# An encoder layer on one core: output projection by 1024 columns, with two of eight pairs of k-tiles as seven products of sums

## The chip, the core and the metric

The kernel runs on one core of one Trainium2 chip. The metric is the device time of one execution in microseconds (us), lower is better. Five engines have instruction streams of their own: PE (matrix products), DVE (elementwise, reads PSUM and SBUF), ACT (activations, copies and casts), POOL (elementwise) and SP (it issues the transfers from memory).

## The reference, cut to what matters

One layer of a hybrid encoder on 256 tokens with 2048 features, all float32:

```python
hn = _rmsnorm(h, norm_w[i])
proj = hn @ w_in[i]                      # 2048 x 18432, nine column groups
q, v, f_fwd, f_bwd, z_a, b_gate, c_gate, h_b, z_b = jnp.split(proj, IN_SPLITS, axis=-1)
o_a = _hgrn2_bidirectional(jax.nn.silu(q), v, f_fwd, f_bwd, lb_all[:, i])
o_a = _head_rmsnorm(o_a, hgrn_norm_w[i]) * jax.nn.silu(z_a)
y_b = b_gate * _short_conv(c_gate * h_b, conv_w[i])
o_b = _rmsnorm(y_b, conv_norm_w[i]) * jax.nn.silu(z_b)
h = h + jnp.concatenate([o_a, o_b], axis=-1) @ w_out[i]      # 4096 x 2048, what is changed
gate = jax.nn.sigmoid(h @ w_ple_gate[i])
h = h + (p[i] @ w_ple[i]) * gate
return _rmsnorm(h, final_norm_w)
```

## The kernel before

**Products.** A float32 product is made of three products of `F32R` parts: each operand is split into a high part (a cast) and a low part (the rest), and high x high, high x low and low x high are summed in PSUM. A weight tile of 128 x 1024 numbers (`raw`, from memory) becomes a tile `spl` of both parts: ACT casts it (`split`, L74), DVE subtracts (L75). There are three `raw` buffers and five `spl` buffers. `Stream` holds the list of weight tiles in the order of use; `get(i)` opens and splits tiles up to three ahead of tile i. A transfer into `raw` waits until the splits of the tile that lay there have ended.

**Stages.** Stage A (groups q, v, f, z_a, up to about 500 us): PE runs the input projections; the gated recurrence of two heads at a time (`mix_forgets`, `mix_pair`) goes on beside them on ACT, DVE and POOL, and PE takes in its small products (`scores`, L506 and L550: `scps`, then `cx`). Calls that are due at a later place among PE's products are put off by `at` and made by `tick`. At the start the tokens are loaded a second time, in another layout (`load_tokens`, L261, into the buffer `xf32`); their squares (`x_squares`, L268 on ACT and L269 on DVE) give the norms, which PE spreads over the partitions (`rps`, L284) and DVE copies to `rbc` (L285). All that POOL does for the recurrence begins with a product by `rbc` (`by_norms`, L346).

Stage B (500 to 841 us) is the short convolution: per pair of channel tiles four projections, then POOL multiplies (`cg*hb`, L684) and ACT and DVE split the result into `mixb` (L695, L696). At its end `turn` transposes the last heads into PSUM tiles `ogt` (tags `y` and `x`); ACT and DVE split them into `mixa` (L437, L438).

Output projection: for each j of four groups of 512 columns `gemm_tok` accumulates `pa` (the half from `mixa`, 16 k-tiles, two row blocks of 128 tokens, three products each) and then `pb` (from `mixb`). DVE adds them to `hh`, which starts as the tokens (L758, L762). `h_transposed` brings the new columns into `ht` for the gate. Then, again by 512 columns, `pp` (per-layer embedding) and `pg` (gate), and the last norm.

PSUM has eight banks: four of pool `psg` with the tag `g`, and four of pool `psm` with the tags `x`, `y`, `sc0`, `sc1`. The order of each engine's instructions is set by the framework's list scheduler from the program's order; `high_priority` pulls instructions ahead.

Of the kernel before, what the change touches and what calls it, by code (L numbers as in the profile page):

```python
# [8 lines left out]
F32 = mybir.dt.float32  # L9
# [8 lines left out]
P = 128  # L18
# [9 lines left out]
class Stream:  # L28
# [11 lines left out]
    def add(self, *srcs):  # L40
# [8 lines left out]
        return list(range(first, len(self.where)))  # L49

    def load(self, j, k0=0, k1=None, pool=None):
        srcs, k, n = self.todo[j]
        if j not in self.raws:
            tag = f"raw{j}" if pool else "raw"
            self.raws[j] = (pool or self.rawp).tile([P, 2048], F32, tag=tag, name=f"raw{j}")
        dst = self.raws[j][:, : k * n].rearrange("p (b k n) -> p b k n", b=len(srcs), k=k)
        for b, src in enumerate(srcs):
            self.nc.sync.dma_start(dst[:, b, k0:k1], src[:, k0:k1])

    def open(self, i):  # L60
        j, h = self.where[i]
        srcs, k, n = self.todo[j]
        if j not in self.raws:
            self.load(j)
        part = self.home[i] if i in self.home else self.splp.tile([P, 2048], F32R, tag="spl", name=f"spl{i}")
        self.parts[i] = part.rearrange("p (k s n) -> p k s n", s=2, n=n)
# [22 lines left out]
def tile_hymba_encoder(  # L89
# [20 lines left out]
    splp = ctx.enter_context(tc.tile_pool(name="splp", bufs=5))  # L110
    xsp = ctx.enter_context(tc.tile_pool(name="xsp", bufs=1))
    psg = ctx.enter_context(tc.tile_pool(name="psg", bufs=4, space=PSUM))
# [20 lines left out]
    for i in range(8):  # L133
        for c in (B_CG, B_HB, B_BG, B_ZB):
            blocks[c, i] = sum((ws.add(w_in[c + i, h]) for h in range(2)), [])
    oblocks = [sum((ws.add(w_out[j, h]) for h in range(8)), []) for j in range(4)]
    gblocks, pblocks = [], []
    for j in range(4):
        pblocks.append(ws.add(w_ple[j]))
        if j < 3:  # L140
            gblocks.append(sum((ws.add(w_gate[j, h]) for h in range(4)), []))
        else:
            halves = [[w_gate_end[b, q // 2, :, 4 * (q % 2) : 4 * (q % 2) + 4] for b in range(2)] for q in range(4)]
            gblocks.append(sum((ws.add(*h) for h in halves), []))


# [506 lines left out]
    for i in range(8):  # L653
# [31 lines left out]
        if i == 0:  # L685
# [40 lines left out]

# [12 lines left out]

    def h_transposed(j):  # L740
        for kk in range(2):
            tp = psm.tile([P, 512], F32, tag="xy"[kk], name=f"ht{j}_{kk}")
            kt = 4 * j + 2 * kk
            for k in range(2):
# [4 lines left out]
            tpv = tp.rearrange("p (k t) -> p k t", k=2)  # L749
            act.copy(out=ht[:, kt : kt + 2, 0, :], in_=tpv)  # L750
            dve.tensor_tensor(out=ht[:, kt : kt + 2, 1, :], in0=tpv, in1=ht[:, kt : kt + 2, 0, :], op=ALU.subtract)

    for j in range(4):
        cs = slice(512 * j, 512 * (j + 1))
        pa = [psg.tile([P, 512], F32, tag="g", name=f"pa{j}_{m}") for m in range(2)]
        gemm_tok(pa, oblocks[j][:8], lambda kt, s: mixa[:, kt, s, :])
        for m in range(2):
            dve.tensor_tensor(out=hh[:, m, cs], in0=pa[m], in1=hh[:, m, cs], op=ALU.add)  # L758
        pb = [psg.tile([P, 512], F32, tag="g", name=f"pb{j}_{m}") for m in range(2)]
        gemm_tok(pb, oblocks[j][8:], lambda kt, s: mixb[:, kt, s, :])  # L760
        for m in range(2):
            dve.scalar_tensor_tensor(  # L762
                out=hh[:, m, cs], in0=pb[m], scalar=rb[:, m : m + 1], in1=hh[:, m, cs], op0=ALU.mult, op1=ALU.add
            )
        at(3, lambda j=j: h_transposed(j))


    mctx.close()
    gp = ctx.enter_context(tc.tile_pool(name="gp", bufs=1, side="right", reuse_waits="tile"))
    fw = gp.tile([P, D], F32, name="fw")  # L770
    nc.sync.dma_start(fw, final_norm_w.rearrange("(o d) -> o d", o=1).broadcast_to([P, D]))
# [48 lines left out]
    for j in range(4):  # L820
        cs = slice(512 * j, 512 * (j + 1))
        pp = [psm.tile([P, 512], F32, tag=("sc0", "sc1")[m], name=f"pp{j}_{m}") for m in range(2)]
        gemm_tok(pp, pblocks[j], lambda kt, s: pt[:, kt, s, :])
        pl = []
        for m in range(2):
            t = gp.tile([P, 512], F32, tag="pl", name=f"pl{j}_{m}", bufs=4)
            act.copy(out=t, in_=pp[m])
            pl.append(t)

        def acc(name):  # L830
            return psg.tile([P, 512], F32, tag="g", name=name)

        if j < 3:
# [78 lines left out]
```

## Time and profile before

| | us |
|---|---|
| median of 3 runs (lowest, highest) | 1128.47 (1127.69, 1128.89) |
| the profiled execution's own time | 1127.79 |
| its span, first to last instruction | 1126.1 |
| PE busy in the span | 1116.5 |
| DVE, ACT, POOL busy | 728.5, 629.4, 217.8 |

The profile is of one execution. A busy time is the sum over an engine's instructions; matrix products overlap at their ends, so a product's duration (0.39 us) is longer than its step from start to start. The mean granted TensorE clock was 0.998 of full.

### The profile page before, as it was taken

What the parts mean: (1) busy time and instruction counts of PE and PEld (TensorE: products, weight loads), DVE (VectorE), ACT (ScalarE), POOL (GpSimd) and SP (SyncE); (2) the same over time, 40 slices, a digit from 0 to 9 for tenths busy, and PEclk for the clock granted to TensorE, in tenths of its full rate; (3) what the DMA queues carried; (4) which work ended last, traced back from release to release, by engine and by line L of the source; (5) the groups of instructions that cost most, each with busy time, mean ns of one, the idle gap of its engine ahead of it and who ended that gap; (6) DMA issues with size and microseconds to landing.
All of it is one profiled execution on the core that took longest, in us unless ns stands there. A gap on an engine that the chain in (4) does not pass through costs nothing.

```text
span 1126.1 us, 16341 instructions
## 1 busy us (share of the span) xinstructions
PE 1116.5 (99%) x6530; PEld 959.9 (85%) x6530; DVE 728.5 (65%) x920; ACT 629.4 (56%) x868; POOL 217.8 (19%) x167
## 2 busy tenths in 40 slices
PE   9999999999999999999999999999999999999996
PEld 8888888888888888888888888888888888888886
DVE  7798476956876587766655665565565555545664
ACT  7696577756775586564454454444445434444553
POOL 1144025300622034221121111121220000000112
PEclk9999999999999999999999999999999999999999
DMA  9746445555545455555555565555557555556542
GB/s 352 268 168 209 155 160 188 159 188 181 201 135 209 163 169 169 192 182 187 188 191 187 182 200 196 194 192 192 188 188 270 187 186 187 187 203 212 201 169 75
DMA packets 37371, 214.25 MB, mean 190 GB/s; under 512 B 4144, under 2 KB 4528, under 8 KB 17584
## 3 DMA queue, kind: packets, MB, share of 16 engines
q1 hardware_dynamic: 37008, 212.88, 54.4%
q8 instruction: 51, 0.84, 0.3%
q10 hardware_dynamic: 288, 0.34, 0.1%
q14 instruction: 24, 0.20, 0.1%
HBM read 211.11 MB, written 2.10 MB: 189 GB/s over the span
## 4 chain that ended last, share of the span: by engine, by line
PE 99%; ACT 0%; DVE 0%; DVEq 0%; issue 0%; ACTq 0%
PE a L309 37%; PE a L307 18%; PE a L330 5%; PE a L328 5%; PE a L329 5%; PE pg L736 3%; PE pg L735 3%; PE pg L737 3%; PE pa L735 3%; PE pa L736 3%; PE pa L737 3%; PE pb L736 3%; PE pb L735 3%; PE pb L737 3%; PE scps L506 1%; PE cx L550 1%
## 5 line engine op out<-in xcount | busy, mean ns | idle before, releaser
L75 DVE TENSOR_TENSOR spl<-raw,spl 128x1024 fp32r<-128x1024 f32 (+2 forms) x398 | 498.5, 1259 | 309.3 <-ACT spl L74 309.1
L309 PE MATMUL a<-xs,spl 128*128 128x512 f32 x1792 | 620.6, 394 | 0.0
L74 ACT CAST spl<-raw 128x1024 fp32r<-128x1024 f32 (+2 forms) x398 | 403.2, 1019 | 329.2 <-PE a L307 164.7
L307 PE MATMUL a<-xs,spl 128*128 128x256 f32 x1792 | 493.2, 278 | 0.0
L309 PEld LDWEIGHTS a<-xs,spl 128*128 128x128 f32 x1792 | 335.0, 188 | 76.9
L307 PEld LDWEIGHTS a<-xs,spl 128*128 128x128 f32 x1792 | 335.9, 188 | 1.9 <-DVE spl L75 0.2
L328 PE MATMUL a<-spl,xs 128*128 128x512 f32 x256 | 100.8, 394 | 0.0
L330 PE MATMUL a<-spl,xs 128*128 128x512 f32 x256 | 99.8, 390 | 0.0
L329 PE MATMUL a<-spl,xs 128*128 128x512 f32 x256 | 99.6, 389 | 0.0
L341 ACT COPY r<-a 128x256 f32<-128x256 f32 x112 | 40.9, 368 | 56.0 <-PE a L307 56.0
L795 POOL TENSOR_TENSOR hh<-hh,fw 128x512 f32<-128x512 f32 (+1 forms) x9 | 11.7, 1311 | 260.4 <-ACT gt L794 257.8
L330 PEld LDWEIGHTS a<-spl,xs 128*128 128x128 f32 x256 | 48.1, 188 | 10.1
L328 PEld LDWEIGHTS a<-spl,xs 128*128 128x128 f32 x256 | 48.1, 188 | 9.6
L329 PEld LDWEIGHTS a<-spl,xs 128*128 128x128 f32 x256 | 48.1, 188 | 9.5
L735 PE MATMUL pa<-spl,mixa 128*128 128x512 f32 x128 | 50.1, 392 | 0.0
L737 PE MATMUL pa<-spl,mixa 128*128 128x512 f32 x128 | 49.8, 389 | 0.0
L736 PE MATMUL pa<-spl,mixa 128*128 128x512 f32 x128 | 49.8, 389 | 0.0
L735 PE MATMUL pb<-spl,mixb 128*128 128x512 f32 x128 | 49.8, 389 | 0.0
L736 PE MATMUL pb<-spl,mixb 128*128 128x512 f32 x128 | 49.8, 389 | 0.0
L737 PE MATMUL pb<-spl,mixb 128*128 128x512 f32 x128 | 49.8, 389 | 0.0
L346 POOL TENSOR_TENSOR xf<-xf,rbc 128x1024 f32<-128x1024 f32 x8 | 19.8, 2477 | 131.1 <-DVE xf L342 124.0
L735 PE MATMUL pg<-spl,ht 128*128 128x512 f32 (+1 forms) x120 | 45.1, 376 | 0.0
(183 smaller groups left out, 1170.6 us busy)
## 6 DMA issues: line engine op xcount, KB each, us to landing
raw<-in_w_in_dram SPq DMA_DIRECT2D x106, 1024.0 KB, 4.9
raw<-in_w_in_dram SPq DMA_DIRECT2D x74, 512.0 KB, 4.9
raw<-in_w_out_dram SPq DMA_DIRECT2D x32, 1024.0 KB, 4.8
raw<-in_w_gate_dram SPq DMA_DIRECT2D x12, 1024.0 KB, 4.8
raw<-in_w_gate_end_dram SPq DMA_DIRECT2D x8, 512.0 KB, 4.8
xf<-in_xtok_dram SPq DMA_DIRECT2D x2, 1024.0 KB, 11.9
hh<-in_xtok_dram SPq DMA_DIRECT2D x1, 2048.0 KB, 8.0
raw<-in_w_ple_dram SPq DMA_DIRECT2D x4, 512.0 KB, 3.4
```

Source lines behind the costliest of these rows:

```text
L74: self.nc.scalar.copy(out=v[:, :, 0], in_=r)
L75: self.nc.vector.tensor_tensor(out=v[:, :, 1], in0=r, in1=v[:, :, 0], op=ALU.subtract)
L307: pe.matmul(a[:, :T], lhsT=lhsT, rhs=xs[:, kt, 0, :], start=False, stop=(kt == NKT - 1))
L309: pe.matmul(a, lhsT=lhsT, rhs=xs[:, kt, :, :].rearrange("p s n -> p (s n)"), start=(kt == 0), stop=False)
L328: pe.matmul(acc[m], lhsT=lh, rhs=w[:, kt % 2, 0, :], start=(kt == 0), stop=False)
L329: pe.matmul(acc[m], lhsT=lh, rhs=w[:, kt % 2, 1, :], start=False, stop=False)
L330: pe.matmul(acc[m], lhsT=ll, rhs=w[:, kt % 2, 0, :], start=False, stop=(kt == NKT - 1))
L341: act.copy(out=r, in_=acc[m][:, 1, :])
L346: pool.tensor_tensor(out=t, in0=t, in1=r.unsqueeze(1).broadcast_to([P, n, T]), op=ALU.mult)
L735: pe.matmul(acc[m], lhsT=lh, rhs=wh, start=(kt == 0), stop=False)
L736: pe.matmul(acc[m], lhsT=lh, rhs=wl, start=False, stop=False)
L737: pe.matmul(acc[m], lhsT=ll, rhs=wh, start=False, stop=(kt == nk - 1))
```

## The change

The output projection goes over two groups u of 1024 columns instead of four of 512. With two row blocks and two column blocks, a pair of k-tiles makes a 2 x 2 by 2 x 2 product of blocks, normally eight block products of three matmuls each. For two of the eight pairs in each half (pairs 2 and 5, `SUMS`) it is computed as seven products of sums of blocks (Winograd's scheme). The sums of weights are made on DVE in the `raw` tile (`sums`), those of `mixa` and `mixb` by `act_sums`. Four of the seven products go to four more PSUM banks, and DVE and ACT combine these after the second such pair. So a half holds all eight banks: `pa` is in `psg` and its extra banks `epa` are in `psm`, for `pb` the other way round.

A weight tile's transfer comes as two of 512 KB instead of one of 1024 KB. `ht` is in two tiles, `xs` is freed before the output projection, and `pr`, `pt` are loaded after `pb`. The first `pp` comes behind the first `pg`. In `Stream.get` the call of `open`, which issues the tile's transfer, now stands inside `high_priority`.

```diff
+    def add_sums(self, *srcs):
+        j = len(self.todo)
+        self.todo.append((srcs, 2, 1024))
+        first = len(self.where)
+        self.where += [(j, h) for h in ("singles", "single", "pairs", "more")]
+        return list(range(first, len(self.where)))
+    def sums(self, j, h):
+        b = self.raws[j].rearrange("p (b n) -> p b n", b=4)
+        add = self.nc.vector.tensor_tensor
+        if h == "singles":
+            return b[:, 0:2]
+        if h == "single":
+            return b[:, 3:4]
+        if h == "pairs":
+            add(out=b[:, 0:3:2], in0=b[:, 0:3:2], in1=b[:, 2:4], op=ALU.add)
+            return b[:, 0:3:2]
+        add(out=b[:, 3], in0=b[:, 0], in1=b[:, 3], op=ALU.add)
+        add(out=b[:, 1], in0=b[:, 3], in1=b[:, 1], op=ALU.add)
+        return b[:, 1:4:2]
...
-                part = self.open(self.next)
                 with self.tc.high_priority(offset=300):
-                    self.split(*part)
+                    self.split(*self.open(self.next))
...
-    oblocks = [sum((ws.add(w_out[j, h]) for h in range(8)), []) for j in range(4)]
+    SUMS = (2, 5)
+    for u in range(2):
+        srcs = [[w_out[2 * u + n, q // 2, :, 2 * (q % 2) : 2 * (q % 2) + 2] for n in range(2)] for q in range(16)]
+        oblocks.append([(ws.add_sums if q % 8 in SUMS else ws.add)(*srcs[q]) for q in range(16)])
...
+    def act_sums(src, dst, a, s):
+        dve.tensor_tensor(out=a, in0=src[:, :, 0], in1=src[:, :, 1], op=ALU.add)
+        a11, a21, a12, a22 = (a[:, k, m * P : (m + 1) * P] for k in range(2) for m in range(2))
+        for o, x, y in ((0, a21, a22), (1, a21, a11), (2, a11, s[:, 0]), (3, a12, s[:, 2])):
+            dve.tensor_tensor(out=s[:, o], in0=x, in1=y, op=ALU.subtract)
+        act.copy(out=dst[:, :, 0], in_=s)
+        dve.tensor_tensor(out=dst[:, :, 1], in0=s, in1=dst[:, :, 0], op=ALU.subtract)
...
+    def half(main, extra, parts, src, sums):
...
+            w = ws.get(ids[0])
+            three(banks[0], *one(0, 0), w[:, 0], st, sp)
+            three(main[0][0], *one(1, 0), w[:, 1], False, False)
+            tick()
+            w = ws.get(ids[1])
+            three(main[0][1], *some(3), w[:, 0], False, False)
+            w = ws.get(ids[2])
+            three(banks[1], *some(0), w[:, 0], st, sp)
+            tick()
+            three(banks[2], *some(1), w[:, 1], st, sp)
+            w = ws.get(ids[3])
+            three(main[1][0], *one(1, 1), w[:, 0], False, False)
+            tick()
+            three(banks[3], *some(2), w[:, 1], st, sp)
+            if sp:
+                yield banks
...
+            for q1, q5, q7, q6 in half([acc[0:2], acc[2:4]], lambda: four(other, "e" + name), parts, src, sums):
+                d, v, d7, v7 = (tmp[:, b] for b in range(4))
+                add_h(0, cs[0], q1, scale)
+                act.copy(out=d, in_=q1)
+                dve.tensor_tensor(out=d, in0=d, in1=q6, op=ALU.subtract)
+                dve.tensor_tensor(out=v, in0=q5, in1=d, op=ALU.subtract)
+                dve.tensor_tensor(out=d7, in0=d, in1=q7, op=ALU.subtract)
+                dve.tensor_tensor(out=v7, in0=v, in1=q7, op=ALU.add)
+                add_h(0, cs[1], v, scale)
+                add_h(1, cs[0], d7, scale)
+                add_h(1, cs[1], v7, scale)
...
+        if j:
+            ple()
         if j < 3:
             pg = [acc(f"pg{j}_{m}") for m in range(2)]
-            gemm_tok(pg, gblocks[j], lambda kt, s: ht[:, kt, s, :])
+            gemm_tok(pg, gblocks[j], lambda kt, s: ht[kt // 8][:, kt % 8, s, :])
+            if j == 0:
+                ple()
```

Three places where the order of instructions differs. **SP, the transfers of the first 60 us**, before: the two token loads stand ahead of the third weight tile of the list that follows the first ones (`raw_541`). "waits" names what a transfer waits for; the DVE waits are for the splits of the tile that lay in the buffer.

```order
L58 DMA raw_515<-in_w_in_dram 128x2048 [waits DMAHW5_49,DVE_49]
L261 DMA xf_80<-in_xtok_dram 128x2048 [waits DMAHW6_49]
L261 DMA xf_80<-in_xtok_dram 128x2048 [waits DMAHW7_49,DMAHW0_49,DVE_49]
L58 DMA raw_541<-in_w_in_dram 128x2048
L58 DMA raw_602<-in_w_in_dram 128x2048 [waits DMAHW4_49,DMAHW1_49,DVE_49]
L58 DMA raw_701<-in_w_in_dram 128x2048 [waits DMAHW5_49,DMAHW2_49,DVE_49]
L58 DMA raw_741<-in_w_in_dram 128x2048 [waits DMAHW3_49,DMAHW0_49,DVE_49]
```

and with the change:

```order
L82 DMA raw_515<-in_w_in_dram 128x2048 [waits DMAHW5_49,DVE_49]
L82 DMA raw_541<-in_w_in_dram 128x2048 [waits DMAHW6_49,DVE_49]
L82 DMA raw_602<-in_w_in_dram 128x2048 [waits DMAHW7_49,DMAHW4_49,DVE_49]
L82 DMA raw_701<-in_w_in_dram 128x2048 [waits DMAHW5_49,DMAHW0_49,DVE_49]
L298 DMA xf_80<-in_xtok_dram 128x2048 [waits DMAHW1_49]
L82 DMA raw_741<-in_w_in_dram 128x2048 [waits DMAHW6_49,DMAHW2_49,DVE_49]
L298 DMA xf_80<-in_xtok_dram 128x2048 [waits DMAHW3_49]
```

Both token loads moved behind later weight tiles: the first behind `raw_701`, the second behind `raw_741`. On PE the two `rps` matmuls, which need the tokens' norms, stand 75 instructions later than before, and the first `scps` 12 matmuls later.

**DVE at the end of stage B**, before (`spl` rows are splits of weights, `mixa<-ogt` the split of the last heads, `mixb` that of the last pair of stage B):

```order
L680 SCALAR_TENSOR_TENSOR hb_7260<-hb_7260,vec,szb_7538 128x256 [waits Activation_49]
L680 SCALAR_TENSOR_TENSOR hb_7260<-hb_7260,vec,szb_7538 128x256 [waits DVE_49]
L75 TENSOR_TENSOR spl_7618<-raw_7601,spl_7618 128x2x512 [waits Activation_49]
L438 SCALAR_TENSOR_TENSOR mixa<-ogt_7554,vec,mixa 128x256 [waits Activation_49]
L707 RECIPROCAL few<-few 128x2 [waits Activation_49]
L708 TENSOR_TENSOR few<-few 128x2 [waits DVE_49]
L75 TENSOR_TENSOR spl_7635<-raw_7633,spl_7635 128x2x512 [waits DMAHW3_49,Activation_49]
L696 TENSOR_TENSOR mixb<-cg_7171,mixb 128x2x256 [waits Activation_49]
L75 TENSOR_TENSOR spl_7650<-raw_7633,spl_7650 128x2x512 [waits Activation_49]
```

and with the change, where L104, L475 and L750 are the old L75, L438 and L696, and L69 to L72 and L685 are sums:

```order
L104 TENSOR_TENSOR spl_7657<-raw_7639,spl_7657 128x512 [waits Activation_49]
L728 SCALAR_TENSOR_TENSOR hb_7279<-hb_7279,vec,szb_7559 128x256 [waits DVE_49]
L71 TENSOR_TENSOR raw_7639<-raw_7639 128x512 [waits DVE_49]
L475 SCALAR_TENSOR_TENSOR mixa<-ogt_7566,vec,mixa 128x256 [waits Activation_49]
L72 TENSOR_TENSOR raw_7639<-raw_7639 128x512 [waits DVE_49]
L750 TENSOR_TENSOR mixb<-cg_7190,mixb 128x2x256 [waits Activation_49]
L104 TENSOR_TENSOR spl_7672<-raw_7639,spl_7672 128x2x512 [waits Activation_49]
L475 SCALAR_TENSOR_TENSOR mixa<-ogt_7575,vec,mixa 128x256
L759 TENSOR_TENSOR few<-few 128x2
L685 TENSOR_TENSOR tmp<-mixb 128x512 [waits DVE_49]
L104 TENSOR_TENSOR spl_7692<-raw_7639,spl_7692 128x2x512 [waits Activation_49]
L475 SCALAR_TENSOR_TENSOR mixa<-ogt_7575,vec,mixa 128x256 [waits Activation_49]
```

The last row that reads `ogt_7575` now stands behind the split of `mixb`, a sum of `mixb` and two more weight splits. **PE there** takes the bank of that `ogt` (tag `x`) for its first extra accumulator:

```order
L798 MATMUL pa_3_7609<-spl_7624,mixa 128x512
L796 MATMUL pa_0_7606<-spl_7642,mixa 128x512
L796 MATMUL epa_x<-spl_7642,mixa 128x512 [waits DVE_49,PE_49]
L797 MATMUL epa_x<-spl_7642,mixa 128x512
L798 MATMUL epa_x<-spl_7642,mixa 128x512
L797 MATMUL pa_0_7606<-spl_7642,mixa 128x512
```

which it enters with the 50th matmul of the projection (twelve for each k-tile of the pairs 0 and 1, and one); before, `pa` used banks of the other pool alone.

**ACT ahead of the first scores**, before (L399 logarithms, L392 a sigmoid, L476 and L477 the exponentials of the first pair of heads):

```order
L474 ACT_TABLE_LOAD
L474 ACTIVATE ge_649<-gx 128x20 [waits DVE_49]
L74 CAST spl_875<-raw_830 128x2x512 [waits PE_49,Activation_49]
L476 ACTIVATE pf_639<-dd_640 128x512 x2
L477 ACTIVATE dd_640<-dd_640 128x512 [waits Activation_49]
L341 COPY r<-a_1_0_768 128x256 [waits PE_49]
L74 CAST spl_893<-raw_890 128x2x512 [waits DMAHW1_49,DMAHW0_49,PE_49]
L341 COPY r<-a_1_1_769 128x256
L477 ACTIVATE dd_640<-dd_640 128x512 [waits Activation_49]
L399 ACT_TABLE_LOAD
```

and with the change (L436, L513, L514 are the old L399, L476, L477):

```order
L511 ACT_TABLE_LOAD
L511 ACTIVATE ge_649<-gx 128x20 [waits DVE_49]
L513 ACTIVATE pf_639<-dd_640 128x512
L103 CAST spl_941<-raw_923 128x2x512 [waits PE_49,Activation_49]
L514 ACTIVATE dd_640<-dd_640 128x512 [waits Activation_49]
L513 ACTIVATE pf_639<-dd_640 128x512
L436 ACT_TABLE_LOAD
L436 ACTIVATE lf_864<-xf_503,lb,oml 128x256
L103 CAST spl_1042<-raw_1039 128x2x512 [waits DMAHW5_49,DMAHW4_49,PE_49]
L514 ACT_TABLE_LOAD
L514 ACTIVATE dd_640<-dd_640 128x512 [waits Activation_49]
```

A logarithm between two table loads and one more weight split moved in ahead of the second exponential of `dd`.

## Rows read from the trace of the kernel before

**Rows 1.** the profile's page: busy time of each engine; the chain that ended last

```profile
PE 1116.5 (99%) x6530; PEld 959.9 (85%) x6530; DVE 728.5 (65%) x920; ACT 629.4 (56%) x868; POOL 217.8 (19%) x167
...
PE 99%; ACT 0%; DVE 0%; DVEq 0%; issue 0%; ACTq 0%
```

**Rows 2.** window of the output projection: busy us (instructions) of each engine, clock, DMA share, GB/s

```profile
841.00:1017.90 176.90, 176.90 (x795) 146.74 (x795) 96.43 (x98) 74.66 (x79) 3.59 (x2) 1.00 0.58 203
```

**Rows 3.** timeline of PE: start, duration, line, operation; in the first pa

```profile
841.30 0.39 PE L736 MATMUL pa<-spl,mixa 128*128 128x512 f32 x1
...
862.63 0.39 PE L737 MATMUL pa<-spl,mixa 128*128 128x512 f32 x1
```

**Rows 4.** groups of instructions, 838 to 1050: busy us, mean ns, idle before, releasers

```profile
L75 DVE TENSOR_TENSOR spl<-raw,spl 128x1024 fp32r<-128x1024 f32 x76 | 93.1, 1225 | 92.4 <-ACT spl L74 92.3
L74 ACT CAST spl<-raw 128x1024 fp32r<-128x1024 f32 x77 | 81.2, 1054 | 110.9 <-PE pb L737 53.3 <-PE pa L737 44.5 <-PE pg L737 11.4
...
L758 DVE TENSOR_TENSOR hh<-pa,hh 128x512 f32<-128x512 f32 x8 | 5.1, 682 | 0.0
...
L827 ACT COPY pl<-pp 128x512 f32<-128x512 f32 x4 | 2.3, 580 | 1.3 <-PE pp L737 1.3
```

**Rows 5.** timeline of POOL, DVE and ACT at the end of stage B

```profile
845.90 2.29 POOL L684 TENSOR_TENSOR cg<-cg,hb 128x512 f32<-128x512 f32 x1 [1.73 <-DVE hb L680]
...
844.88 0.88 DVE L680 SCALAR_TENSOR_TENSOR hb<-hb,vec,szb 128x256 f32<-128x256 f32 x2 [0.29 <-ACT szb L677]
...
846.96 0.48 DVE L438 SCALAR_TENSOR_TENSOR mixa<-ogt,vec,mixa 128x256 fp32r<-128x256 f32 x1
...
849.88 0.68 DVE L696 TENSOR_TENSOR mixb<-cg,mixb 128x512 fp32r<-128x512 f32 x1
...
848.60 0.62 ACT L695 CAST mixb<-cg 128x512 fp32r<-128x512 f32 x1
```

**Rows 6.** source line 684: durations min/median/max, first and last start

```profile
L684 POOL TENSOR_TENSOR cg<-cg,hb x8: 1292/1297/2292, 535.4 to 845.9; 128x512 f32<-128x512 f32 x8
```

**Rows 7.** timeline of SP's queue and DVE; DMA issues with median us to landing

```profile
19.70 9.24 SPq L261 DMA_DIRECT2D xf<-in_xtok_dram  x2
...
39.12 1.23 DVE L75 TENSOR_TENSOR spl<-raw,spl 128x1024 fp32r<-128x1024 f32 x1 [0.60 <-ACT spl L74]
...
xf<-in_xtok_dram SPq DMA_DIRECT2D x2, 1024.0 KB, 11.9
```

**Rows 8.** timeline of DVE, ACT, POOL and PE from the norms to the first scores

```profile
45.20 1.28 ACT L276 ACT_TABLE_LOAD   x1 [0.84 <-DVE few L275]
46.50 0.29 ACT L276 ACTIVATE few<-few,epst 128x2 f32<-128x2 f32 x1
...
52.98 0.41 DVE L285 COPY rbc<-rps 128x256 f32<-128x256 f32 x1
...
50.20 0.40 PE L309 MATMUL a<-xs,spl 128*128 128x512 f32 x1
...
50.55 0.60 PE L284 MATMUL rps<-ident,rw 128*128 128x128 f32 x4
...
53.49 2.40 POOL L346 TENSOR_TENSOR xf<-xf,rbc 128x1024 f32<-128x1024 f32 x1 [7.05 <-DVE rbc L285]
...
55.92 1.06 ACT L390 ACTIVATE xf<-xf 128x1024 f32<-128x1024 f32 x1 [0.71 <-POOL xf L346]
...
62.50 1.09 ACT L399 ACTIVATE lf<-xf,lb,oml 128x256 f32<-128x256 f32 x2
...
82.17 0.67 POOL L487 TENSOR_TENSOR kc<-dd,ge 128x256 f32<-128x256 f32 x1
82.93 1.91 POOL L493 TENSOR_TENSOR kx<-kc,ge 128x512 f32<-128x512 f32 x1
...
86.97 0.30 PE L506 MATMUL scps<-qc,dd 128*32 128x128 f32 x2
...
88.24 1.16 PE L550 MATMUL cx<-qc,kx 128*128 128x128 f32 x8
```

More of the change, by code (lines that the diff above doesn't have):

```diff
@@ L65, in open @@
         part = self.home[i] if i in self.home else self.splp.tile([P, 2048], F32R, tag="spl", name=f"spl{i}")
+        if isinstance(h, str):
+            r = self.sums(j, h)
+            nb = r.shape[1]
+            self.parts[i] = part[:, : nb * 1024].rearrange("p (b s n) -> p b s n", b=nb, s=2)
+            return r, self.parts[i]
         self.parts[i] = part.rearrange("p (k s n) -> p k s n", s=2, n=n)
@@ L693, in tile_hymba_encoder @@
                 act.copy(out=og[:, e], in_=kept[e])
+        if i in (4, 5):
+            a = bp.tile([P, 2, T], F32, tag="sa", name=f"sa{i}")
+            b = bp.tile([P, 4, P], F32, tag="sb", name=f"sb{i}")
+            k = 2 * SUMS[i - 4]
+            act_sums(mixa[:, k : k + 2], suma[:, i - 4], a, b)
         hi, lo = mixb[:, 2 * i : 2 * i + 2, 0, :], mixb[:, 2 * i : 2 * i + 2, 1, :]
@@ L749, in h_transposed @@
             tpv = tp.rearrange("p (k t) -> p k t", k=2)
[L750 to L765, printed above, removed]
+            dst = ht[u][:, kt % 8 : kt % 8 + 2]
@@ new lines, in h_transposed, with four, add_h @@
+            act.copy(out=dst[:, :, 0, :], in_=tpv)
+            dve.tensor_tensor(out=dst[:, :, 1, :], in0=tpv, in1=dst[:, :, 0, :], op=ALU.subtract)
+    def four(pool_, name):
+        if pool_ is psg:
+            return [psg.tile([P, 512], F32, tag="g", name=f"{name}_{b}") for b in range(4)]
+        return [psm.tile([P, 512], F32, tag=t, name=f"{name}_{t}") for t in ("x", "y", "sc0", "sc1")]
+    def add_h(m, cs, v, scale):
+        h = hh[:, m, cs]
+        if scale:
+            dve.scalar_tensor_tensor(out=h, in0=v, scalar=rb[:, m : m + 1], in1=h, op0=ALU.mult, op1=ALU.add)
+        else:
+            dve.tensor_tensor(out=h, in0=v, in1=h, op=ALU.add)
@@ new lines, in tile_hymba_encoder @@
+    for u in range(2):
+        cs = [slice(512 * (2 * u + n), 512 * (2 * u + n + 1)) for n in range(2)]
+        for src, sums, main, other, scale in ((mixa, suma, psg, psm, False), (mixb, sumb, psm, psg, True)):
+            name = f"p{'ab'[scale]}{u}"
+            acc = four(main, name)
+            parts = oblocks[u][8 * scale : 8 * scale + 8]
+            if u == 0 and not scale:
+                for z in range(2):
+                    k = 2 * SUMS[z]
+                    act_sums(
+                        mixb[:, k : k + 2], sumb[:, z], tmp[:, 0:1].rearrange("p b (k t) -> p (b k) t", k=2),
+                        tmp[:, 1:2].rearrange("p b (o t) -> p (b o) t", o=4),
+                    )
+            for q1, q5, q7, q6 in half([acc[0:2], acc[2:4]], lambda: four(other, "e" + name), parts, src, sums):
[9 more added lines that the diff above has]
+                add_h(1, cs[1], v7, scale)
+            with tc.high_priority(offset=200):
+                for m in range(2):
+                    for n in range(2):
+                        add_h(m, cs[n], acc[2 * m + n], scale)
+        for z in range(2):
+            at(5 + 2 * z, lambda u=u, z=z: h_transposed(u, z))
@@ L768, in tile_hymba_encoder @@
     mctx.close()
+    sctx.close()
+    hp2 = ctx.enter_context(tc.tile_pool(name="hp2", bufs=1, side="left", reuse_waits="tile"))
+    ht.append(hp2.tile([P, NKT // 2, 2, T], F32R, name="ht1"))
     gp = ctx.enter_context(tc.tile_pool(name="gp", bufs=1, side="right", reuse_waits="tile"))
+    pr = gp.tile([P, 2, T], F32, name="pr")
+    nc.sync.dma_start(pr, pt_in)
+    pt = gp.tile([P, 2, 2, T], F32R, name="pt")
+    act.copy(out=pt[:, :, 0, :], in_=pr)
+    dve.tensor_tensor(out=pt[:, :, 1, :], in0=pr, in1=pt[:, :, 0, :], op=ALU.subtract)
```

72 lines of the change are left out of this document (52 added, 20 removed).

## The prediction

> **What bounds the kernel now.** The page comes first: PE is busy 1116.5 of 1126.1 us, and the chain that ended last is 99% PE [rows 1]. So every matmul that goes is worth its step, and every time PE has to wait is lost whole; nothing else counts. Then the window of the output projection: PE is busy in all of its 176.9 us at full granted clock, DVE for 96 and ACT for 75 [rows 2]. The timeline gives a matmul's step: from the second of the first `pa` at 841.30 to its 96th at 862.63 it is 21.33 / 94 = 0.227 us (the row's 0.39 overlaps the next) [rows 3]. Last the groups: DVE's splits wait 92 us for ACT's casts, and these wait for PE to give back a `spl` buffer [rows 4]. The splits therefore run as far ahead as five buffers let them. DVE and ACT have room there.
>
> The profiled execution took 1127.79 us, 0.68 less than the median of the runs. I make the sum against its rows and add 0.68 at the end.
>
> **What is removed.** A pair of k-tiles with two row and two column blocks takes 24 matmuls as eight block products (three matmuls each) and 21 as seven. A half of 1024 columns has two such pairs, and there are four halves (`pa`, `pb`, twice), eight pairs in all: 24 of 768 matmuls go, 24 x 0.227 = **5.44 us** [rows 3]. The transposes for the gate and the products behind it stay as many.
>
> **What is added and hidden.** A pair of sums costs DVE three sums (one over 1024 columns as the split's 1.23, two over 512 at 0.68) and splits over 3584 columns instead of 2048 (three of 1.23 and one of 0.68): 6.96 us, while PE needs 21 x 0.227 = 4.76 for it [rows 3, 4]. It is 2.2 us too much for DVE, but a normal pair needs 2.46 of DVE's time in 5.44 of PE's, so the two pairs behind it give back 6; and the splits begin four tiles ahead, some 11 us at twelve matmuls each. Combining the extra banks (eight DVE operations of 0.68, one copy on ACT) takes 5.5 us once in a half, and two more pairs follow before the other half's extra banks want those banks. Over a half DVE has about 39 of 42 us to do. I cost this at nothing; if the order breaks this cover, DVE is the bound there, a rival below. The transfers are the same bytes in halves, at nothing too, since the DMA share in the window was 0.58 [rows 2]. `pr` and `pt` come behind `pb`, but their first user now stands behind the first `pg`, 96 matmuls or 21.8 us later; nothing again.
>
> **First seam: the bank of `x`.** The pieces of order show the new wait. `epa_x` is entered with matmul 50, nominally at 841.07 + 49 x 0.227 = 852.2 [rows 3]. Its bank holds `ogt_7575` until DVE's last row on it, in before done at 847.44 [rows 5] and now last of twelve rows. Followed along the rows: `L728` ends some 0.7 later than the old L680 at 845.76, since a split of 512 columns stands between its two, so POOL's product starts at 846.5 instead of 845.90. With 2.29 it ends at 848.8; ACT's cast to `mixb` 0.62, 849.4; ACT's cast of `spl_7672` 1.05, 850.5. DVE: its split 1.23, 851.7; `mixa` 0.48; a small one; the sum 0.68; the split of `spl_7692` 1.23; `mixa` 0.48: 854.7, or 854.3 with the 0.1 by which rows in a queue overlap [rows 4, 5]. PE waits **2.1 us**. In seven of eight cases that POOL product took 1.30 and not 2.29 [rows 6]; with it the wait is 1.1. I take the long one, because it is the same place of the program with DVE still busier. The Trainium skill ("GPSIMD Engine Reference", section 1, Specifications) says that GpSimd shares its SBUF interfaces with VectorE and contends with DVE instructions that have two SBUF inputs. This trace agrees: the one long case is the one beside a weight split. By that rule the sum stands as it is, without it 1.0 us lower.
>
> **Early: the token loads.** In the order of SP they fall behind `raw_701` and `raw_741`, whose transfers wait for splits: issued from 19.70 on before [rows 7], now the first behind the split that ends at 40.35 [rows 7], the second two PE tiles (16 products, 8 x 0.35 = 2.8 each [rows 8]) later, about 46.4. With the landing of 11.9 [rows 7] the tokens are there by 58.3. On ACT the table load for the square root now stands behind a weight cast whose buffer PE gives back at about 59.9: cast to 60.9, load of 1.28 to 62.2, square root 0.29 [rows 8]; on DVE the reciprocal, an evacuation and two copies to `rw` of about 0.4 each then end at about 63.9, an estimate. PE comes to `rps`, 75 instructions later than at 50.55, at 50.55 + 37 x 0.35 = 63.5: a wait of **0.4 us**. But `rbc`, which DVE had at 53.39 [rows 8], comes at 66.2 (PE, then a weight split and an evacuation ahead of it on DVE). Everything that leads to the first scores begins with it, and those moved on PE by 12 matmuls only.
>
> The cover was 3.4 us: `kx` ended at 84.84, `cx` began at 88.24 [rows 8]. Now `scps` is nominally at 86.97 + 12 x 0.227 + 0.4 = 90.1, `cx` at 91.4. The chain: POOL's product of `xf` 2.40, to 68.7. Then ACT's queue up to the second exponential of `dd`: seven casts of 1.05, five table loads of 1.28, two sigmoids of 1.06, five activations over 512 columns and five logarithms at about 0.6, three small ones, 22.9 in all; less 0.1 at a dozen places, since two logarithms together took 1.09 [rows 4, 8]. That is 90.2. DVE's product 0.68 gives `dd` at 91.0, so the scores wait 0.9; POOL's `kc` and `kx` of 0.67 and 1.91 [rows 8] end at 93.6, when `cx` stands at 92.3, so 1.3 more. I take **2.2 us**. The bounds: no wait, if the chain is 2 us shorter than its rows; 6.3 if it keeps the 31.45 us that it took before from `rbc` to `kx` (66.2 + 31.45 = 97.65 against 91.4). It lies nearer the lower, since before part of the 31.45 was waiting for PE's products, which are done by now. The second pair follows with the same delay, **0.3 us** (0 to 1).
>
> One more thing speaks against this stretch. After a table load the next activation began 0.02 us behind its end [rows 8]; I cost a load at its row. The Trainium skill ("ScalarE: Activation LUTs", What ACT_TABLE_LOAD costs) gives 1283 ns and a drain of about 1380 ns more for a switch. The row agrees with the first figure and shows no second; with it, by that page, five switches would add 6.9 us.
>
> **The gate's seam.** The first `pp` comes behind `pg`, and the second `pp` takes its banks soon after: ACT must copy both (0.58 each [rows 4]) with a sigmoid and a weight cast between, in a queue that starts when PE is done. I take **0.4 us** (0 to 1).
>
> **Sum.** -5.44 + 2.1 + 0.4 + 2.2 + 0.3 + 0.4 = -0.04, so 1127.8 by the profile and 1128.4 by the median. What PE saves it waits for elsewhere.
>
> **The rivals.**
> 1. *The full gain*: no stall outlasts its cover. For it: ACT and DVE have idle time all along, and 2 to 3 us less on either chain are enough. Against: both chains run through queues in which each row is at its known duration. -5.44, 1123.0.
> 2. *Only the early chain is in time*: the first seam stays with 2.1, with 0.4 and 0.4: 1125.9.
> 3. *The early chain keeps its old length*: the stall there is 6.3 and not 2.2: 1132.5, slower. It decides from 1.9 us more than I took. POOL's products of 3 us beside DVE's splits would do it.
> 4. *DVE becomes the bound in the pairs of sums*: if a half's DVE work of 39 us is split badly around the 42 us of PE, about 1 us in each of four halves is waited for: 1132.4.
> 5. *Table loads cost more than their rows*: the 0.84 us ahead of the load [rows 8] is put down to DVE; if it belonged to the load, five make 4.2 us, 1132.6. The page "ScalarE: Activation LUTs" of the Trainium skill (What ACT_TABLE_LOAD costs), weighed above, would have it so.
>
> **How the numbers follow.** My forecast has 0.45, the full gain 0.17, the second 0.13, the third 0.17, the fourth 0.06, the fifth 0.02. The forecast's own range is 1126.5 to 1131.5 (stalls of 3.5 to 8.5 us). The whole range goes from 1122.8, the full gain, to 1133.0. About 0.2%, 2.26 us, is what a measurement of this kernel can tell from no change: below 1126.2 is faster, above 1130.7 slower. Faster: 0.17, half of the second and a tenth of the forecast, 0.29. Slower: 0.25 from the last three and a tenth of the forecast, 0.30. The same: 0.41.
>
> **What would show it.** PE's waits, of which before had one (at the start): new ones on DVE at `epa_x` about 852 to 854, on POOL and DVE at the first `scps` and `cx`, on DVE at `rps`. `rbc` at 66 instead of 53. The output projection in 171.3 us plus its stall. If DVE's idle time in the window is near zero and PE waits for splits there, the fourth rival holds. The prediction is wrong if PE shows no wait at 852 or at 90, or if waits stand where none is named here: in the pairs of sums, or at the later seams, which I cost at nothing.

## The result, and the profile after

The changed kernel took 1130.78 us in the median of ten runs (1129.51 to 1133.0), the kernel before 1127.83 (1126.82 to 1128.89). The ratio is 1.0026, with a 95% interval of 1.0017 to 1.0036: slower by 2.95 us. The profiled execution after took 1129.86 us with a span of 1128.1, which is 2.07 and 2.0 more than before.

The page of the changed kernel, busy time of each engine and the chain that ended last:

```profile
PE 1113.0 (99%) x6506; PEld 956.2 (85%) x6506; DVE 785.0 (70%) x1016; ACT 646.9 (57%) x893; POOL 214.4 (19%) x167
...
PE 95%; DVE 2%; ACT 1%; POOL 1%; issue 0%; DMA 0%; DVEq 0%; ACTq 0%; POOLq 0%
```

PE's waits in it (who ended the wait: us in total, times, the longest):

```profile
PE scps L543 <- DVE dd L515: 2.9, 1, 2.9
PE epa_x L796 <- DVE mixa L475: 2.3, 1, 2.3
...
PE a L346 <- DVE xs L287: 0.5, 1, 0.5
```

PE is busy 3.5 us less than before [rows 1], and its chain fell from 99% to 95%: other engines now hold it up. Two long waits stand in the list, at the two places that the prediction named, one at the first scores and one at the first extra bank. The wait of 0.5 lies at the start of the kernel, and as the first product began 0.05 us earlier than before it cost nothing that shows.

The first scores of the changed kernel, in windows (columns as in [rows 2]):

```profile
89.90:93.00 3.10, 0.22 (x1) 0.00 (x0) 3.10 (x4) 3.06 (x5) 2.15 (x3) 1.00 0.58 197
93.00:95.30 2.30, 2.26 (x80) 2.24 (x80) 0.92 (x2) 2.28 (x4) 1.74 (x2) 0.53 0.00 0
95.30:97.00 1.70, 1.70 (x15) 1.69 (x10) 1.70 (x4) 1.19 (x2) 0.42 (x1) 0.64 0.14 24
```

The timeline of SP's queue there:

```profile
40.57 0.42 SPq L298 DMA_DIRECT2D xf<-in_xtok_dram  x1
...
46.23 0.42 SPq L298 DMA_DIRECT2D xf<-in_xtok_dram  x1
```

The timeline of DVE:

```profile
65.72 0.42 DVE L322 COPY rbc<-rps 128x256 f32<-128x256 f32 x1
...
90.02 1.21 DVE L104 TENSOR_TENSOR spl<-raw,spl 128x1024 fp32r<-128x1024 f32 x1
91.15 1.75 DVE L515 TENSOR_TENSOR dd<-xf,dd 128x512 f32<-128x512 f32 x1
```

The timeline of ACT:

```profile
90.10 0.63 ACT L514 ACTIVATE dd<-dd 128x512 f32<-128x512 f32 x1
```

The timeline of POOL:

```profile
90.23 2.11 POOL L383 TENSOR_TENSOR qt<-qt,rbc 128x512 f32<-128x512 f32 x1 [0.33 <-DVE qt L379]
...
93.77 1.05 POOL L530 TENSOR_TENSOR kx<-kc,ge 128x512 f32<-128x512 f32 x1
```

The timeline of PE:

```profile
93.04 0.34 PE L543 MATMUL scps<-qc,dd 128*32 128x128 f32 x2 [2.92 <-DVE dd L515]
...
95.31 1.01 PE L587 MATMUL cx<-qc,kx 128*128 128x128 f32 x3
```

The token loads go out at 40.57 and 46.23, `rbc` is ready at 66.14 instead of 53.39 [rows 8], and ACT ends the second exponential of `dd` at 90.73. Then DVE still has a weight split ahead (90.02) and takes 1.75 us for the product that makes `dd`, beside POOL's product of 2.11. PE stands still for 2.9 us. And one thing more: in the window behind the wait the granted clock is 0.53 in the mean: nearly all of it at the lower of TensorE's two levels, 1.2 GHz and not 2.4. From the first scores to `cx` PE needs 2.27 us, 1.27 before [rows 8], and 1.49 from `cx` to the next product, 0.92 before.

The seam, where the extra bank of `x` is entered, in the timeline of POOL:

```profile
847.58 2.21 POOL L383 TENSOR_TENSOR hb<-hb,rbc 128x512 f32<-128x512 f32 x1 [6.90 <-DVE hb L379]
852.23 1.60 POOL L732 TENSOR_TENSOR cg<-cg,hb 128x512 f32<-128x512 f32 x1 [2.44 <-DVE hb L728]
```

The timeline of DVE there:

```profile
853.00 1.38 DVE L72 TENSOR_TENSOR raw<-raw 128x512 f32<-128x512 f32 x1
...
855.47 1.23 DVE L104 TENSOR_TENSOR spl<-raw,spl 128x1024 fp32r<-128x1024 f32 x1 [0.26 <-ACT spl L103]
...
857.07 0.68 DVE L685 TENSOR_TENSOR tmp<-mixb 128x512 f32<-128x512 f32 x1
857.67 1.21 DVE L104 TENSOR_TENSOR spl<-raw,spl 128x1024 fp32r<-128x1024 f32 x1
858.81 0.47 DVE L475 SCALAR_TENSOR_TENSOR mixa<-ogt,vec,mixa 128x256 fp32r<-128x256 f32 x1
```

The timeline of PE there:

```profile
859.43 0.47 PE L796 MATMUL epa_x<-spl,mixa 128*128 128x512 f32 x1 [2.34 <-DVE mixa L475]
```

The window behind PE's wait:

```profile
859.40:862.00 2.60, 2.57 (x11) 2.17 (x12) 2.57 (x8) 2.43 (x4) 0.00 (x0) 1.00 0.76 210
```

All of it is 4.7 us later than in before, as the early loss is carried on. The last reader of `ogt_7575` is the row at 858.81, and PE goes on 0.2 behind its end. Here the clock stays at 1.00 after the wait.

The output projection of the changed kernel as one window:

```profile
845.70:1018.90 173.20, 170.86 (x763) 141.38 (x763) 148.59 (x177) 87.95 (x98) 3.82 (x2) 1.00 0.61 206
```

The timeline of PE at its begin:

```profile
845.68 0.48 PE L796 MATMUL pa<-spl,mixa 128*128 128x512 f32 x1
```

The timeline of PE at its end:

```profile
1018.63 0.39 PE L798 MATMUL pb_sc<-spl,mixb 128*128 128x512 f32 x1
1018.86 0.39 PE L789 MATMUL pg<-spl,ht 128*128 128x512 f32 x1
```

The waits from there to the gate, of which PE's weight loads have one:

```profile
PEld pp L789 <- ACT pl L973: 0.4, 2, 0.2
```

From the first `pa` to the last `pb` PE takes 172.95 us, before 176.64 (840.99 to 1017.63). DVE is busy 149 of 173 us, before 96 of 177 [rows 2], and yet PE waits for no split in the pairs of sums.

| term, us | predicted | in the profile | how |
|---|---|---|---|
| 24 matmuls | -5.44 | -5.40 | 172.95 - 2.50 wait + 0.79 for eight transposes that now lie behind, less 176.64 |
| early: `rps`, scores, second pair | +2.9 | +4.69 | first `pa` at 845.68 instead of 840.99 |
| of it the wait at the scores | 0.9 | 2.98 | 3.30 between neighbours instead of 0.32 |
| of it scores and `cx` | 1.3 | 1.57 | 1.00 and 0.57, at the lower clock |
| first seam | +2.1 | +2.50 | 2.73 between neighbours less a step of 0.23 |
| gate's seam and the rest | +0.4 | +0.2 | what is left of +2.0 in the span |

PE came to the first scores 0.4 us later than twelve more products account for (89.74 + 0.32, against 86.97 + 12 x 0.227). The prediction put such a 0.4 down to a wait at `rps`, but PE's list names no wait there. The timeline of PE at `rps`:

```profile
63.26 0.39 PE L346 MATMUL a<-xs,spl 128*128 128x512 f32 x1
63.60 0.46 PE L321 MATMUL rps<-ident,rw 128*128 128x128 f32 x2
```

From such a product to the next it is 0.23 elsewhere, here 0.34, so PE stood still for 0.1 and no more. The 0.4, 2.98 and 1.57 make 4.95, 0.26 more than the shift of `pa`. Where the rest of the 0.4 was lost and the 0.26 won back is not placed.

### The profile page after: what moved, and what is told of

Read it like the earlier page. It is cut to its first block, busy times and chain, and to the rows that moved or that the text cites. A ratio compares the mean times of both kernels' runs of the same rounds, so it can differ in the third digit from the quotient of the medians.

```text
span 1128.1 us, 16505 instructions
## 1 busy us (share of the span) xinstructions
PE 1113.0 (99%) x6506; PEld 956.2 (85%) x6506; DVE 785.0 (70%) x1016; ACT 646.9 (57%) x893; POOL 214.4 (19%) x167
## 4 chain that ended last, share of the span: by engine, by line
PE 95%; DVE 2%; ACT 1%; POOL 1%; issue 0%; DMA 0%; DVEq 0%; ACTq 0%; POOLq 0%
PE a L346 36%; PE a L344 18%; PE a L367 5%; PE a L366 5%; PE a L365 5%; PE pg L790 3%; PE pg L789 3%; PE pg L791 3%; PE pa L798 2%; PE pa L797 2%; PE pa L796 2%; PE pb_sc L798 1%; PE pb_sc L797 1%; PE pb_sc L796 1%; PE scps L543 1%; DVE spl L104 1%
## 5 line engine op out<-in xcount | busy, mean ns | idle before, releaser
L104 DVE TENSOR_TENSOR spl<-raw,spl 128x1024 fp32r<-128x1024 f32 (+2 forms) x414 | 510.2, 1242 | 250.2 <-ACT spl L103 249.2
L103 ACT CAST spl<-raw 128x1024 fp32r<-128x1024 f32 (+2 forms) x414 | 415.8, 1011 | 313.0 <-PE a L344 171.1
L789 PE MATMUL pg<-spl,ht 128*128 128x512 f32 (+1 forms) x120 | 45.2, 377 | 0.0
L790 PE MATMUL pg<-spl,ht 128*128 128x512 f32 (+1 forms) x120 | 45.1, 375 | 0.0
L791 PE MATMUL pg<-spl,ht 128*128 128x512 f32 (+1 forms) x120 | 45.0, 375 | 0.0
L383 POOL TENSOR_TENSOR xf<-xf,rbc 128x1024 f32<-128x1024 f32 x8 | 20.4, 2556 | 123.1 <-DVE xf L379 117.8
L524 POOL TENSOR_TENSOR qc<-pf,ge 128x256 f32<-128x256 f32 x16 | 32.8, 2051 | 50.2 <-DVE pf L516 29.2
L796 PE MATMUL pa<-spl,mixa 128*128 128x512 f32 x104 | 40.7, 392 | 0.0
L798 PE MATMUL pa<-spl,mixa 128*128 128x512 f32 x104 | 40.5, 389 | 0.0
L797 PE MATMUL pa<-spl,mixa 128*128 128x512 f32 x104 | 40.5, 389 | 0.0
```

The costliest lines, as they stand in the source:

```text
L103: self.nc.scalar.copy(out=v[:, :, 0], in_=r)
L104: self.nc.vector.tensor_tensor(out=v[:, :, 1], in0=r, in1=v[:, :, 0], op=ALU.subtract)
L789: pe.matmul(acc[m], lhsT=lh, rhs=wh, start=(kt == 0), stop=False)
L790: pe.matmul(acc[m], lhsT=lh, rhs=wl, start=False, stop=False)
L791: pe.matmul(acc[m], lhsT=ll, rhs=wh, start=False, stop=(kt == nk - 1))
L796: pe.matmul(acc, lhsT=ah, rhs=w[:, 0], start=start, stop=False)
```

## The experiments

**1. One line undone.** The transfer is issued ahead of `high_priority` again, the split stays inside.

```diff
+                j = self.where[self.next][0]
+                if j not in self.raws:
+                    self.load(j)
                 with self.tc.high_priority(offset=300):
                     self.split(*self.open(self.next))
```

> The changed kernel with one line undone: the weight tile's transfer is issued outside high_priority as before the change, the split stays inside. Theory (the token loads, pushed back on SP's queue, make the first scores late; PE waits 2.9 us and then runs 1.6 us longer at the lower granted clock): rbc is ready at 53 again, the early 4.7 us go, the wait of 2.3 at the first extra bank stays, so about 1126.1, some 1.7 us below the kernel before. Rival (the loss comes from the sums and the grouping by 1024 columns): stays at 1130.8.

Measured: 1126.41 us, ratio to before 0.9986 (0.9977 to 0.9994), 4.4 us below the changed kernel. The first scores begin at 86.79, with no wait, and the first `pa` at 840.81. The seam is as it was.

PE's waits of this kernel:

```profile
PE epa_x L799 <- DVE mixa L478: 2.3, 1, 2.3
...
PE a L349 <- ACT spl L103: 0.4, 1, 0.4
```

So one line with nothing to do with the sums, moved by a line's indentation, made the changed kernel slower than before.

**2. That line alone.** The kernel before with `open` inside `high_priority`, nothing else.

```diff
-                part = self.open(self.next)
                 with self.tc.high_priority(offset=300):
-                    self.split(*part)
+                    self.split(*self.open(self.next))
```

> The kernel before with that one line of the change alone (open inside high_priority), no sums, no grouping. Theory: the early loss appears by itself, 1127.8 + 4.7 = 1132.5, with rbc at 66 and a wait of some 3 us at the first scores, followed by a stretch at about half the granted clock. Rival (the early delay needs the other parts of the change, or is a matter of that one execution): 1127.8, no wait at the first scores.

Measured: 1132.82 us, ratio 1.0043 (1.0030 to 1.0056), +5.0.

PE's waits of it:

```profile
PE scps L505 <- DVE dd L477: 2.8, 1, 2.8
```

The windows behind the wait (columns as in [rows 2]):

```profile
93.00:96.00 3.00, 2.67 (x82) 2.53 (x83) 1.62 (x3) 2.98 (x4) 1.77 (x2) 0.59 0.00 0
96.00:98.00 2.00, 2.00 (x12) 1.87 (x12) 2.00 (x5) 1.39 (x3) 1.11 (x1) 0.76 0.37 109
```

The wait of 2.8 and the lower clock behind it appear without the sums. The rival is refuted.

**3. The tokens ahead.** The changed kernel with the two token loads inside `high_priority(offset=600)`.

```diff
 def load_tokens(m):
-    nc.sync.dma_start(...)
+    with tc.high_priority(offset=600):
+        nc.sync.dma_start(...)
```

> The changed kernel, only the two token loads are given a high priority too, so that they stand ahead of the weight tiles on SP's queue again; the weights' transfers stay inside high_priority. Theory (it is the lateness of the tokens): as with the line undone, about 1126.1. Rival (the earlier issue of the weights does the harm, by crowding ACT and DVE in that stretch): the wait at the first scores stays, 1130 or so.

Measured: 1126.96 us, ratio 0.9994 (0.9985 to 1.0003). The first scores begin at 87.83 without a wait. It is the tokens' place in the queue; issuing the weights early does no harm that these runs can tell when the tokens go ahead (0.55 us over experiment 1, inside both spreads).

**4. Another order of the extra banks.** The changed kernel; in the first half `sc1`, `sc0`, `y`, `x`.

```diff
-        return [psm.tile(... tag=t ...) for t in ("x", "y", "sc0", "sc1")]
+        tags = ("sc1", "sc0", "y", "x") if name == "epa0" else ("x", "y", "sc0", "sc1")
+        return [psm.tile(... tag=t ...) for t in tags]
```

> The changed kernel, only the order of the four extra banks of the first half differs: sc1, sc0, y, x instead of x, y, sc0, sc1, so that the bank with the last transposed heads is entered with matmul 67 and not 50. Theory: the wait of 2.3 at the seam goes; PE then comes to the splits behind it earlier, of which the first ends only 1.8 us ahead of its use now, so up to 0.7 us comes back there: 1128.3 to 1129.0. Rival (DVE's queue as a whole is late there, the bank is only where it shows): PE waits as long for the splits behind, gain under 0.5, 1130.5.

Measured: 1128.78 us, ratio 1.0005 (0.9997 to 1.0014), 2.0 us below the changed kernel.

PE's waits of it:

```profile
PE scps L543 <- DVE dd L515: 2.9, 1, 2.9
...
PE cx L587 <- POOL kx L530: 0.5, 2, 0.3
PE pa L797 <- DVE spl L104: 0.4, 1, 0.4
```

The window behind the wait at the scores:

```profile
93.00:95.30 2.30, 1.82 (x81) 1.48 (x82) 0.92 (x3) 2.28 (x4) 1.77 (x2) 1.00 0.00 0
```

The wait for the bank is gone; 0.4 us of it come back as a wait for a split, as expected. The early wait is the same 2.9, but here the clock behind it is 1.00. `cx` then waits 0.5 for POOL's `kx` instead. So the lower clock in the first profile cost about 1.1 us net (1.57 less this 0.5), in that execution.

**5. Both repairs.** Edits 1 and 4 together.

> The changed kernel with both repairs: the transfer outside high_priority and the order of the extra banks. Theory: the two losses are in different places and add up, so 1130.8 - 4.4 - 2.0 = 1124.4; on PE only about 0.4 us of waits for a split at the seam and 0.5 at the gate are left of the losses. Rival (one loss covers the other, DVE's queue at the seam comes out late by itself): 1126.

Measured: 1124.32 us, ratio 0.9968 (0.9955 to 0.9980). The two losses add up: by the ratios of experiments 1 and 4 it would be 0.9965.

PE's only wait behind the start:

```profile
PE pa L800 <- DVE spl L104: 0.4, 1, 0.4
```

**6. The gate's seam.** Edit 5, and `pp` of j = 1 in the banks `x` and `y`.

```diff
-tag=("sc0", "sc1")[m]
+tag=("xy" if j == 1 else ("sc0", "sc1"))[m]
```

> The former kernel, and the second embedding product pp of j = 1 in the banks x and y instead of sc0 and sc1. Theory: PE's wait for ACT's copies at the gate (0.4 us) goes, 1124.0. Rival (PE waits there for something else, or the copies are late anyway by the same amount): 1124.4.

Measured: 1123.34 us, ratio 0.9959 (0.9947 to 0.9972), the fastest of all. The weight loads' wait for `pl` (0.4 us in the changed kernel) is gone from the list. But from the first to the last `pg` PE takes 100.68 us, against 100.77 in the former kernel: 0.1 us. The medians differ by 1.0, the profiled executions not at all (1123.63 and 1123.51), and the intervals of the two kernels overlap. So the 1.0 may be chance; it stays open, and I count 0.1. The rival, that the copies are late anyway, is not refuted.

**7. One pair of sums in a half, and 8. none.** Edit 6 with `SUMS = (5,)`, and with `SUMS = ()` and the temporary tiles left out.

> The former kernel with one pair of sums in a half (pair 5) instead of two. Theory (a pair of sums is worth its three matmuls, 0.68 us, four times, and costs PE nothing): 1124.0 + 2.7 = 1126.7. Rival (the sums' work on DVE makes PE wait, so that a pair is worth less): 1124.5 to 1125.5; if a pair costs more than it gives, under 1124.

> The same kernel with no pair of sums at all: the grouping by 1024 columns, the halved transfers, the late pr and the two parts of ht alone. Theory: as many matmuls as before and nothing that PE waits for: 1127.8, the kernel before; by the difference to the kernel with two pairs 3.8 to 5.4. Rival (grouping or halved transfers cost something by themselves): 1128.5 to 1130.

Measured: 1125.59 us with one (0.9978, 0.9969 to 0.9987) and 1128.58 with none (1.0002, 0.9993 to 1.0011). From two to one it is 2.25 us, from one to none 2.99, together 5.24 of the 5.44 that the matmuls are worth. But these differences rest on the 1123.34 of experiment 6, with its open 1.0 us. The traces are firmer: from the first `pa` to the last `pb` PE takes 171.03 us with two pairs (841.45 to 1012.48), 173.07 with one (841.21 to 1014.28) and 175.77 with none (841.92 to 1017.69). So pair 5 alone gives 2.70, all that its matmuls are worth, and pair 2 with it only 2.04. Most of the missing 0.68 is at the seam. With two pairs PE waits there for a split (0.54 between two neighbours, 857.20 and 857.97, beyond a step); with one it doesn't wait. The expectation of 2.7 for a pair is missed by that, the rival's 0.5 to 1.5 as well.

The grouping by 1024 columns and the halved transfers cost nothing that these runs can tell. The 1128.58 lies in the rival's range, but the kernel before took 1128.13 beside it; PE has no wait behind the start, and its 175.77 are the 176.64 of before less the 0.79 for eight transposes, within 0.1.

**9 and 10. Two more profiles.** The kernel of experiment 1 and the changed kernel, one more profiled execution each, since their runs spread over 3.4 and 3.5 us, and those of the kernels without long waits (experiments 5 to 8) over 0.8 to 2.2.

> One more profiled execution of the kernel with the transfer outside high_priority (its eleven times spread over 3.4 us, at mean granted clocks of 0.996 to 0.999, and its profile is of one of the shortest). Theory: PE's wait of 2.3 us at the first extra bank is followed in some executions by a stretch at about half the granted clock, and these are the longer ones; where this execution is above 1126 us, the windows behind 859 or another wait show such a stretch, and where it is near 1125 they show none. Rival (the waits themselves differ from execution to execution): the wait at the bank is longer or shorter than 2.3 by as much as the time differs.

> One more profiled execution of the changed kernel itself. Theory: the two waits (3 us at the first scores, 2.3 to 2.5 at the first extra bank) are as long as in the first profile; what differs is the stretch at about half the granted clock behind either, none, one or both, worth about 1 to 1.6 us each, which is why the median lies 0.9 above the profiled execution. Rival: the waits differ.

Measured: 1125.81 and 1132.43 us.

PE's waits in the changed kernel's second profile:

```profile
PE scps L543 <- DVE dd L515: 2.8, 1, 2.8
PE epa_x L796 <- DVE mixa L475: 2.3, 1, 2.3
PE a L346 <- ACT spl L103: 1.5, 1, 1.5
```

Windows of it, two at the scores and one behind the bank:

```profile
93.30:95.30 2.00, 0.72 (x29) 0.48 (x30) 1.46 (x2) 1.99 (x5) 1.31 (x2) 1.00 0.05 20
95.30:98.00 2.70, 2.50 (x63) 2.31 (x64) 1.86 (x3) 2.67 (x4) 1.05 (x1) 1.00 0.00 0
...
860.00:864.00 4.00, 3.64 (x11) 3.00 (x12) 3.97 (x10) 3.61 (x5) 0.00 (x0) 0.70 0.73 217
```

The two waits are as long as before, 2.8 and 2.3. This time the clock stays at 1.00 behind the scores and falls behind the bank, to 0.70 in the mean of the window: eight products there take 0.42 each instead of 0.23, 1.6 us. Another 1.5 us were waited for the first weights at the start (0.5 in the first profile). The first profile had its dip behind the scores instead, and 1.0 us less at the start. The second profile of experiment 1's kernel showed no dip; its 0.8 us over the first profile of that kernel come at the start, where it waited 0.9 for a split and not 0.4. For the changed kernel the theory holds in that the waits were the same and the dip moved; that dips make its median is not shown. In the other kernel it wasn't put to the test.

## Why the prediction was wrong

It forecast 1128.4 us and no change, and the kernel became slower by 2.95 us. The 1130.78 lies inside the forecast's own range, near its upper end (1131.5). The mechanisms stood at their places; sizes were off, nearly all in one term.

**What PE saves: right.** -5.44 forecast, -5.40 in the trace. **What was costed at nothing: right.** No wait in the pairs of sums of the changed kernel, none at the later seams, no cost of the halved transfers (experiment 8) or of `pr`.

**The first seam: right, a little small.** 2.1 forecast, 2.5 measured. In the working DVE and POOL began as in before; but POOL's product ahead (`L383`) took 2.21 and not the 1.30 that the row had at the same place. The timeline of POOL there, before:

```profile
842.88 1.30 POOL L346 TENSOR_TENSOR hb<-hb,rbc 128x512 f32<-128x512 f32 x1 [6.90 <-DVE hb L342]
```

The timeline of DVE there, with the change:

```profile
847.41 1.21 DVE L69 TENSOR_TENSOR raw<-raw 128x1024 f32<-128x1024 f32 x1
```

POOL's product of 2.21 began at 847.58, beside this sum. The long `cg*hb` of 2.29, on which I had staked a microsecond, took 1.60. The two errors go against each other, so it is partly luck that the sum came out within 0.4. A sum on DVE took 1.38 and not 0.68, but the split behind it (855.47) waited for ACT, not for DVE. Experiment 4 shows that the bank was what PE waited for, and 0.4 of the 2.5 that DVE's queue would have been late anyway.

**The early chain: the step that failed.** The text took 2.2 us at the first scores, from `dd` at 91.0 and `kx` at 93.6. `rbc` was forecast for 66.2 and came at 66.14; the second exponential was forecast for 90.2 and ended at 90.73. Up to there it held within 0.5. Then "DVE's product 0.68 gives `dd` at 91.0" failed: DVE first ended a weight split at 91.2, and the product took 1.75, to 92.90. So the wait at the scores was 2.98 and not 0.9. Of the 1.9 by which `dd` was late, 1.1 are the product's length.

I took the 0.68 that such a product has where POOL does nothing [rows 4] and put it where POOL ran a product of its own. But POOL's running alone doesn't make the difference. The same product of `dd` in before, in the timeline of DVE:

```profile
80.39 0.68 DVE L478 TENSOR_TENSOR dd<-xf,dd 128x512 f32<-128x512 f32 x1
```

The timeline of POOL there, before:

```profile
80.61 1.61 POOL L346 TENSOR_TENSOR qt<-qt,rbc 128x512 f32<-128x512 f32 x1 [0.33 <-DVE qt L342]
```

There it took 0.68 although POOL's product began 0.22 behind it, and POOL's was the longer one, with 1.61 instead of 1.30. With the change POOL's product (90.23) began beside DVE's split (90.02) and took 2.11, and DVE's product (91.15) began beside POOL's and took 1.75. In all three pairs the row that began later was lengthened, and it ended roughly its own length behind the end of the other: 92.34 + 0.68 is 93.02, against 92.90. POOL's 2.21 at the seam, begun 0.17 behind DVE's sum, is a fourth. So what the sum lacked was whose turn it was: some 11 us later than before, the second product of `dd` met POOL's product already running. The page "GPSIMD Engine Reference" of the Trainium skill (section 1, Specifications), which the prediction cites for POOL's side, says that POOL contends with DVE instructions that have two SBUF inputs; this trace agrees on DVE's side too, with 1.75 us where the same product took 0.68 before. Experiments 2 and 4 and the second profile of the changed kernel have the product at 1.74 to 1.75 again. This is read from the rows; no run moved one of the two products alone.

The 1.3 us for `kx` came out near (1.57), by luck: `kx` ended at 94.82 and `cx` began at 95.31, so PE didn't wait for `kx` in this execution, but ran at the lower clock. Where the clock stayed up (experiment 4), the wait for `kx` was 0.5.

Two smaller slips changed nothing. The terms of ACT's queue add up to 90.4, not 90.2. The token loads landed in 6.9 us, not 11.9; the table load for the square root stood behind a weight cast all the same.

**The granted clock: not foreseen.** The prediction worked with one clock throughout. Behind PE's wait it was at the lower level in some executions: behind three of nine waits of 2.3 to 3 us in the profiles here (the changed kernel's first profile at the scores, its second at the bank, experiment 2 at the scores), at 1.1 to 1.6 us each where it can be told. In the other six it stayed. The Trainium skill ("TensorE: Matmul & The Clock Gate", Part 1: The HAM clock gate) says that the point at which the clock rises under sustained matmuls varies from run to run. The runs here show as much of the fall: behind the same wait at the same place it came once and not the other time. Whether it explains part of the 0.9 us by which the median lies over the profiled execution is not shown: that execution had a dip itself, and of the ten runs only it has a trace.

**The rivals.** The first (full gain) is what the repaired kernel shows: 1124.32 and 1123.34 against 1123.0 forecast. The third was on the right side, slower by the early chain, but not by its own mechanism: the chain from `rbc` to `kx` took 28.68 us (66.14 to 94.82), against 27.4 in the forecast and 31.45 by this rival, and the lengthened row that counted was DVE's beside POOL's. Of its 6.3 us for the scores, 4.55 were measured (2.98 and 1.57). The second (only the early chain in time) was forecast at 1125.9 and is experiment 1: 1126.41. The fourth is refuted by the absence of waits for splits; once the bank is out of the way, 0.4 us of such a wait shows at the seam (experiment 4). The fifth: after each table load the next activation follows within 0.05 us, five times in this chain; no further cost.

## What to carry to other kernels

A change is more than the lines that it is for: the order of the transfers' queue moved by an edit that reads as tidying, and one line cost 5 us, as much as all the sums gave. Compare the order of every queue, follow what became late to the engine that sets the end, and add up the chain with the lengths that rows have beside the same neighbours. For products of DVE and POOL that run together, as in these traces, ask which one begins first: the other one was the longer. Where a new accumulator takes a bank, choose the bank whose last reader ends first: that was four fifths of the loss at the seam, for another order of four names.

## What the runs showed of the hardware that was not expected

After a wait of PE of 2.8 to 2.9 us the granted clock was 0.53 to 0.59 in the next window in two executions and 1.00 in two others; after a wait of 2.3 it fell once in five. A wait's price is so its length and, by chance, 1.1 to 1.6 us more. It may be what widens the spread, 3.5 us over ten runs with two such waits against 2.1 over 21 runs of the kernel before; only one of the ten has a trace. And a DVE product over 128x512 float32 took 1.75 us when it began beside a running POOL product; begun 0.22 us ahead of one it took 0.68, and POOL's took 1.61 instead of 1.30.
